# A one-layer diffusion backbone: the opening's sums between its modulation slabs, and linear-attention levels that follow half chunks of weights

## The chip, the cores and the metric

The kernel runs on one core of one Trainium2 chip. A core has a matrix engine (TensorE, PE in the profile; its weight loads are PEld), a vector engine (DVE), a scalar engine (ACT), a general one (GpSimd, POOL) and an engine that mainly issues transfers (SP), and 16 DMA engines. Each engine works through its own queue of instructions in order; semaphores make one wait for another. The metric is the device time of one execution in microseconds (us), and less is better. Before the change it is 1974.27 us, the median of three runs (1974.04 to 1974.33).

## What is computed

One layer for 256 latent tokens and 256 context tokens, 2048 wide, in float32. The reference, cut to what matters here:

```python
mod_x = jnp.split((jax.nn.silu(c) @ w_mod[l] + b_mod[l])[:, None, :], 6, axis=-1)
mod_c = jnp.split((jax.nn.silu(c_ctx) @ w_mod[l] + b_mod[l])[None, None, :], 6, axis=-1)
qa, ka, va, qb, kb, vb, rb, gf, gb, gate_a, gate_b = proj(modulate(x, g_mix[l], mod_x[0], mod_x[1]))
...
o_attn = windowed_attention(qa, ka, va, cka, cva, attn_sink[l])
sf, sb, o_gla_c = context_gla(cqb, ckb, cvb, cgf, cgb, need_out=not last)
o_gla = latent_gla(qb, kb, vb, gf, gb, sf, sb)
x = x + mod_x[2] * merge_branches(o_attn, o_gla, ...)
x = x + mod_x[5] * conv_ffn(modulate(x, g_ffn[l], mod_x[3], mod_x[4]), ...)
```

`modulate` is an RMS norm times (1 + scale) plus shift, and shift and scale come out of `c @ w_mod`. The linear attention (GLA) has 4 heads with 256 key and 512 value channels each, runs in both directions, and decays by log-sigmoid gates (`gf`, `gb`) that are low-rank projections of the normed input.

## The kernel before, in words

**Products.** Each float32 weight is split into a high part (`whi`, on ACT, L211) and a low part (`wlo`, on DVE, L212); activations are split likewise (`h00hi`, `h00lo`: latent tokens, first half of the channels; `h10hi`: context tokens; `h01hi`, `h11hi`: second half). A product is high·high, low·high and high·low. Weights are loaded 1024 columns by 128 rows at a time, a *chunk* of 512 KB (`raw`); a block of projection goes over 16 row tiles in 8 chunks, in `proj_nat` (L222) or `proj_T` (L263). In each chunk PE first runs the products with `whi`, then those with `wlo`.

**Places.** Ahead of a chunk's high part the program calls `tick()` (L171), and ahead of its low part `midway()` (L164) or a function `mid` given in its stead. So a block of 8 chunks has 16 places at which other work is put into PE's queue. A generator in `beside` is stepped there by `aside()` (L156) at a given rate, and small background steps (`bg_steps`) at another. While a place is worked off, `pin` ties its matmuls into PE's order at that place; the order on DVE, ACT and POOL is made by a scheduler with its own model of durations.

**The opening (L538 to L600).** A slab of `w_mod` (`mraw`, 1 MB) is multiplied with the two modulation vectors (`pm`, 32 rows in use), the result is transposed on DVE (`mtr`), turned back into columns by a product (`pcol`), and copied and summed into `scale` or `shift`. `mod_both` (L313) makes such steps: for the first group a0 and a1 are the two slabs of the scale and ea its columns; b0, b1 and eb are those of the shift. `square_sums` (L431) forms the squares of the tokens (`sq`) on ACT and DVE, and `add_up` sums them over channels with a product with ones (`pr`). `factor_row` (L466) makes the norm's factor (`vrow`, `rrow`) of it, `affine_scale` (L497) multiplies tokens, scale and factor into `xr`, and `affine_shift` (L506) adds the shift and splits into `h..hi` (ACT) and `h..lo` (DVE). `idle(n)` (L533) puts n transposes of a constant into PE's queue, whose results nobody reads. The channels come in five groups of 2, 2, 4, 4 and 4 row tiles: (0, 2), (2, 2), (4, 4), (8, 4), (12, 4), and in the loop from L616 each group's normed input goes at once into the blocks QB, KB and VB (partial sums in `qb0`, `kb`, `vb`), while the next groups' slabs are multiplied. In group 1 the function `mid` does so by the list `steps` (how many slab steps each of its six calls takes) and the list `also` (which columns or scales are finished there). SP issues these loads in the order of the program.

**The linear attention (`gla_A`, L740).** For a head four *gate pieces*: a product `pz`, on ACT an absolute value, a relu, an exp and a log (L756 to L760), a sum on DVE (L761, into `segs`) and one on POOL (L762, `gc`). Then eight levels of doubling segments: ACT makes exponentials of the running sums (L829, L830, L836, L837), DVE multiplies them with the head's `q` and `k` (L831, L838) and extends the sums (L840 to L843), and PE multiplies the level before (`pa<-q,k`), which DVE writes into `at` by a mask (L814). Beside some levels stand scans and products for `kf` and `kg` (L770 to L789). At the end two more `q` (L857), the product `pa<-q,kf` and its eviction (`atc`). `with_gla` (L905) steps the whole generator, 4 gate pieces, 8 levels and the end, at rate 0.97 beside the 16 places of a block, which puts the gate pieces at places 1 to 4 and the levels from place 5 on: the block KB for head 0, and a value block (`v_block`) for heads 1 to 3. `gla_o` then multiplies with the values (`po`).

## Time and profile before

| | |
|---|---|
| median of three runs | 1974.27 us (1974.04 to 1974.33) |
| the profiled execution | 1973.72 us, of which the profile's span 1972.0 us |
| PE busy in the span | 99%, 10304 instructions |
| DVE / ACT / POOL busy | 71% / 49% / 2% |
| moved by DMA | 420.90 MB, mean 213 GB/s |
| granted clock of PE | 1.00 |

In a row of a line view stand the start and the length in us, the engine, the line of the kernel, the operation, what it writes and reads, the shapes, how many rows were merged, and in brackets how long the engine stood idle before and for whom. Where one row reads x16 for 8 products of the program, a float32 product that isn't split runs as two passes. Ends of matmuls are modelled, so two starts tell more than an end and a start. Idle time of an engine that nobody waits for costs nothing.

### The profile page before, as it was taken

How to read it: one execution, taken by the hardware profiler on the slowest of the kernel's cores; microseconds unless marked ns; L12 is line 12 of the kernel's file. 1: busy time of each engine (PE TensorE's matmuls, PEld its weight loads, DVE VectorE, ACT ScalarE, POOL GpSimd, SP SyncE). 2: the span in 40 equal slices, each digit the busy share in tenths (PEclk: the TensorE clock that was granted, in tenths of full speed). 3: DMA queues.
4: the chain of work that ended last, by engine and by line, in shares of the span. 5: the costliest groups of instructions: out<-in, count | busy, mean ns of one | idle time of the engine just before them, and what ended most of it. 6: DMA issues, size and time to landing. Idle time of an engine off the chain costs nothing.

```text
span 1972.0 us, 27091 instructions
## 1 busy us (share of the span) xinstructions
PE 1952.8 (99%) x10304; PEld 1635.6 (83%) x10304; DVE 1396.9 (71%) x2150; ACT 971.6 (49%) x1415; POOL 39.9 (2%) x60
## 2 busy tenths in 40 slices
PE   8999999999999999999999999999999999999999
PEld 6679988888887777888888888888888888888887
DVE  5756855785768998777776467989886545677754
ACT  5223655462346565444444445755555334555533
POOL 0010000020000000000000000000000000000000
PEclk9999999999999999999999999999999999999999
DMA  9975222226654466899997677688786556666563
GB/s 392 412 255 176 69 66 71 79 84 210 212 162 126 129 208 220 297 299 307 312 310 237 238 246 252 193 276 284 263 275 224 192 193 191 186 188 191 188 212 114
DMA packets 182867, 420.90 MB, mean 213 GB/s; under 512 B 12512, under 2 KB 12736, under 8 KB 177744
## 3 DMA queue, kind: packets, MB, share of 16 engines
q1 hardware_dynamic: 181200, 413.45, 63.7%
q0 software_dynamic: 1360, 5.54, 1.0%
q8 instruction: 81, 1.33, 0.3%
q14 instruction: 50, 0.41, 0.1%
q10 hardware_dynamic: 176, 0.17, 0.0%
HBM read 416.98 MB, written 2.13 MB: 213 GB/s over the span
## 4 chain that ended last, share of the span: by engine, by line
PE 94%; DVE 3%; ACT 1%; DMA 1%; issue 1%; ACTq 0%; DVEq 0%
PE acc L83 72%; PE accs L83 12%; PE pa L95 2%; PE poa L95 1%; PE pS L95 1%; PE po L95 1%; PE pm L95 1%; DVE wlo L212 1%; PE ptp L98 1%; DMA mraw<-in_w_mod 1%; ACT whi L211 0%; DVE q L831 0%; PE pto L98 0%; DMA pack<-in_k_pack 0%; DVE k L838 0%
## 5 line engine op out<-in xcount | busy, mean ns | idle before, releaser
L212 DVE TENSOR_TENSOR wlo<-raw,whi 128x1024 fp32r<-128x1024 f32 x568 | 694.0, 1223 | 426.5 <-ACT whi L211 387.8
L211 ACT ACTIVATE whi<-raw 128x1024 fp32r<-128x1024 f32 x568 | 601.1, 1059 | 785.1 <-PE acc L83 605.0
L83 PE MATMUL accs<-h,whi 128*128 128x512 f32 x704 | 176.3, 392 | 0.0
L83 PE MATMUL acc<-h,whi 128*128 128x512 f32 x640 | 160.4, 392 | 0.0
L83 PEld LDWEIGHTS accs<-h,whi 128*128 128x128 f32 x704 | 126.6, 189 | 22.6
L83 PE MATMUL acc<-whi,h01hi 128*128 128x512 f32 x352 | 139.7, 397 | 0.0
L83 PE MATMUL acc<-whi,h00hi 128*128 128x512 f32 x352 | 139.2, 395 | 0.0
L83 PE MATMUL acc<-whi,h01lo 128*128 128x512 f32 x352 | 138.4, 393 | 0.0
L83 PE MATMUL acc<-whi,h00lo 128*128 128x512 f32 x352 | 137.6, 391 | 0.0
L83 PE MATMUL acc<-whi,al 128*128 128x512 f32 x352 | 137.0, 389 | 0.0
L83 PE MATMUL acc<-whi,ah 128*128 128x512 f32 x352 | 137.0, 389 | 0.0
L83 PEld LDWEIGHTS acc<-h,whi 128*128 128x128 f32 x640 | 115.1, 189 | 20.6
L83 PEld LDWEIGHTS accs<-h,wlo 128*128 128x128 f32 x704 | 96.0, 190 | 6.9
L83 PE MATMUL acc<-wlo,h01hi 128*128 128x512 f32 x352 | 99.0, 396 | 0.0
L83 PE MATMUL accs<-h,wlo 128*128 128x256 f32 x704 | 98.2, 282 | 0.0
L83 PE MATMUL acc<-wlo,h00hi 128*128 128x512 f32 x352 | 98.1, 394 | 0.0
L83 PE MATMUL acc<-wlo,ah 128*128 128x512 f32 x352 | 94.3, 389 | 0.0
L83 PEld LDWEIGHTS acc<-h,wlo 128*128 128x128 f32 x640 | 87.4, 190 | 6.3
L83 PE MATMUL acc<-h,wlo 128*128 128x256 f32 x640 | 89.4, 282 | 0.0
L376 DVE CUSTOM_DVE_ANT_0 raw<-raw,csrow,pack 128x1024 f32<-128x1024 f32 x64 | 81.2, 1278 | 0.0
L83 PEld LDWEIGHTS acc<-whi,al 128*128 128x128 f32 x352 | 66.1, 188 | 13.7
L83 PEld LDWEIGHTS acc<-whi,ah 128*128 128x128 f32 x352 | 66.1, 188 | 13.7
(376 smaller groups left out, 3553.0 us busy)
## 6 DMA issues: line engine op xcount, KB each, us to landing
raw<-in_w_in SPq DMA_DIRECT2D x204, 512.0 KB, 4.5
raw<-in_w_up SPq DMA_DIRECT2D x176, 512.0 KB, 4.2
raw<-in_w_modT SPq DMA_DIRECT2D x128, 512.0 KB, 4.6
raw<-in_w_down SPq DMA_DIRECT2D x88, 512.0 KB, 3.6
mraw<-in_w_mod SPq DMA_DIRECT2D x30, 1024.0 KB, 12.5
raw<-in_w_attn_o SPq DMA_DIRECT2D x32, 512.0 KB, 5.3
raw<-in_w_gla_o SPq DMA_DIRECT2D x32, 512.0 KB, 5.4
raw<-in_w_out SPq DMA_DIRECT2D x32, 512.0 KB, 4.4
```

The source lines that it names most:

```text
L83: r = pe_seq(PE.matmul(*a, **k))
L95: return pe_seq(after(PE.matmul(*a, **k)))
L98: return pe_seq(after(PE.transpose(*a)))
L211: j = S.activation(hi[:, 0:n, :], raw[:, 0:n, :], AF.Copy).ins
L212: i = V.tensor_tensor(lo[:, 0:n, :], raw[:, 0:n, :], hi[:, 0:n, :].bitcast(F32), op=ALU.subtract).ins
L376: i0 = V.tensor_tensor_reduce(out=raws[i], in0=raws[i], in1=row[0], scale=1.0, scalar=d if h else bmod[:, b0:b0 + 1], op0=ALU.mult, op1=AL ...
```

## The change

Four edits.

1. `mod_both` loads every slab in one transfer; before, the second slab of a first part was loaded in two halves for the first four row tiles.
2. In the opening the products of slab a0 come after four of the nine sums, those of a1 after six, and the factor after all nine. `idle` runs with 10, 2, 4 and 8 transposes instead of 10, 6, 4, 6, 4 and 8. The small `gm1` is tied behind the first square on DVE.
3. In group 1 the list of steps reads 1, 2, 1, 3, 1, 0 instead of 1, 2, 1, 4, 0, 0, and the columns of group 2's shift are finished in the sixth `mid`, ahead of `affine_shift`, instead of the fifth.
4. `gla_A` is split into `gla_gates(h)`, the four gate pieces, and the levels. A table names what stands at each of the 16 places. Head 0: its gates at 0 to 3, levels at 4 and 6 to 13 (the ninth of these steps is the last level's product and the two last `q`), the end at 15. Other heads: their last two gates at 0 and 1, levels at 2, 4, 5, 7, 8, 10, 11, 12 and 13, the end at 15. The next head's first two gate pieces stand at 9 (13 beside head 0) and 14. In the changed file the lines behind the first edit have numbers that differ by a few.

```diff
--- before.py
+++ after.py
@@ -320,12 +320,7 @@
             if k0 == 0:
                 a.append(bank(f"pm{part}_{t0}", (P, w), side=True))
             raw = M("mraw", [P, nk, w])
-            src = A["w_mod01"][part, t0 + k0 // nk].rearrange("p (c d) -> p c d", c=nk)
-            if t0 < 4 and part == 0 and k0:
-                load(raw[:, 0:nk // 2, :], src[:, 0:nk // 2, :])
-                load(raw[:, nk // 2:nk, :], src[:, nk // 2:nk, :])
-            else:
-                load(raw, src)
+            load(raw, A["w_mod01"][part, t0 + k0 // nk].rearrange("p (c d) -> p c d", c=nk))
             for k in range(nk):
                 kt = k0 + k
                 q = 32 * (kt % 4)
@@ -428,6 +423,8 @@
     kbt = M("kb0", [P, 4, 512])
     vb0 = M("vb0", [P, 4, 512])
 
+    squared = []
+
     def square_sums(s):
 
         pr = bank("pr", (P, T), side=True)
@@ -440,7 +437,7 @@
                 if s and i in (0, 2):
                     in_order(evicted[i + 1], j)
             else:
-                V.tensor_tensor(q, x_, x_, op=ALU.mult)
+                squared.append(V.tensor_tensor(q, x_, x_, op=ALU.mult).ins)
                 parts.extend(q[:, k, :] for k in range(4))
                 continue
             h = q[:, 0:2, :]
@@ -538,19 +535,18 @@
     opening[:] = [pe_seq(PE.transpose(warm[:, 0:P], ident, ident)).ins]
     idle(10)
     pr, add_up = square_sums(0)
-    add_up(0, 6)
-    V.tensor_scalar(gm1, gmix, -0.5, None, op0=ALU.mult)
+    add_up(0, 4)
+    in_order(squared[0], V.tensor_scalar(gm1, gmix, -0.5, None, op0=ALU.mult).ins)
     (a0, a1, ea), (b0, b1, eb) = mods[0]
+    a0()
+    add_up(4, 6)
+    a1()
     add_up(6, 9)
     factor_row(pr)
-    a0()
-    idle(6)
-    a1()
-    idle(4)
     ea()
     b0()
     affine_scale(0, *groups[0])
-    idle(6)
+    idle(2)
     b1()
     raws = [first_w(i) for i in range(2)]
     idle(4)
@@ -628,7 +624,7 @@
             bg_rate[:] = [1.4 * len(bg_steps) / ticks + 0.01, 0.0]
             if gi == 1:
                 bg_rate[:] = [0.0, 0.0]
-                steps = iter([1, 2, 1, 4, 0, 0])
+                steps = iter([1, 2, 1, 3, 1, 0])
 
                 def next_columns():
                     if pend:
@@ -639,7 +635,11 @@
                     for s in range(2):
                         affine_scale(s, *groups[2])
 
-                also = iter([next_columns] * 3 + [scale_2, next_columns, lambda: affine_shift(0, *groups[2])])
+                def shift_2():
+                    next_columns()
+                    affine_shift(0, *groups[2])
+
+                also = iter([next_columns] * 3 + [scale_2, next_columns, shift_2])
 
                 def mid():
                     pin[0] = last[0]
@@ -737,16 +737,13 @@
                          b.rearrange("p (f t) -> p f t", f=2), AF.Copy, scale=1.0 / 16)
         return eq
 
-    def gla_A(h, kb, qb, res):
-        k_ = kb[:, (h % 2) * 2:(h % 2) * 2 + 2, 0:T]
-        kc = kb[:, (h % 2) * 2:(h % 2) * 2 + 2, T:2 * T]
-        q_ = qb[:, 2 * h:2 * h + 2, :]
+    def gla_gates(h):
         R = M("segs", [P, 4, 2, T])
-        PF, SB, SX, PX = (R[:, i] for i in range(4))
         G.memset(R[:, 2:4], 0.0)
         gc = []
+        yield R, gc
         for d in range(2):
-            g_ = W2("fc", "gc", [P, 2, T])
+            gc.append(W2("fc", "gc", [P, 2, T]))
             for dt in range(2):
                 f = 2 * h + dt
                 pz = bank("pz", side=True)
@@ -758,11 +755,15 @@
                 S.activation(mn, pz, AF.Relu, scale=-1.0, bias=b)
                 S.activation(e, e, AF.Exp, scale=-1.0)
                 S.activation(e, e, AF.Ln, bias=ones[:, 0:1])
-                V.tensor_tensor((PF if d == 0 else SB)[:, dt, :], mn[:, 0:T], e[:, 0:T], op=ALU.add)
-                G.tensor_tensor(g_[:, dt, :], mn[:, T:2 * T], e[:, T:2 * T], op=ALU.add)
+                V.tensor_tensor(R[:, d, dt, :], mn[:, 0:T], e[:, 0:T], op=ALU.add)
+                G.tensor_tensor(gc[d][:, dt, :], mn[:, T:2 * T], e[:, T:2 * T], op=ALU.add)
                 yield
-            gc.append(g_)
-
+
+    def gla_A(h, kb, qb, R, gc, res):
+        k_ = kb[:, (h % 2) * 2:(h % 2) * 2 + 2, 0:T]
+        kc = kb[:, (h % 2) * 2:(h % 2) * 2 + 2, T:2 * T]
+        q_ = qb[:, 2 * h:2 * h + 2, :]
+        PF, SB, SX, PX = (R[:, i] for i in range(4))
         kf = W2("fb", "kf", [P, 2, T])
         kg = W2("fb", "kg", [P, 2, T])
 
@@ -856,7 +857,6 @@
             S.activation(dst, e, AF.Exp, scale=-1.0 / 16)
             V.tensor_tensor(dst, dst, q_, op=ALU.mult)
         yield
-        yield
         pa = bank("pa", (P, 2, T), side=True)
         for t in range(2):
             for i, (kk, qq) in enumerate(((kf, q2), (kg, q3))):
@@ -902,9 +902,38 @@
     for i in range(4):
         q_evac(i // 2)(i % 2, qb0[i])
 
+    gates = {}
+
+    def gate(h):
+        if h == 4:
+            return
+        if h not in gates:
+            it = gla_gates(h)
+            gates[h] = next(it), it
+        next(gates[h][1])
+
     def with_gla(h, kb, block):
-        res = []
-        beside[:] = [gla_A(h, kb, qbt, res), 0.97, 0.0]
+        res, own = [], []
+
+        def level():
+            if not own:
+                own.append(gla_A(h, kb, qbt, *gates[h][0], res))
+            next(own[0], None)
+
+        this, following = lambda: gate(h), lambda: gate(h + 1)
+        places = {i: [this] for i in ((0, 1, 2, 3) if h == 0 else (0, 1))}
+        for i in (4, 6, 7, 8, 9, 10, 11, 12) if h == 0 else (2, 4, 5, 7, 8, 10, 11, 12):
+            places[i] = [level]
+        places.update({13: [level], 14: [following], 15: [level]})
+        places.setdefault(13 if h == 0 else 9, []).append(following)
+
+        def along():
+            for i in range(16):
+                for fn in places.get(i, ()):
+                    fn()
+                yield
+
+        beside[:] = [along(), 1.0, 0.0]
         v = block()
         for _ in beside[0]:
             pass
```

How the edits move instructions, at three places. First PE's queue in the opening, from the first transposes of a constant (`warm`) to the second slab of the shift; `pr` is a sum of squares, the two `pm` names are scale (first) and shift. Before:

```order
L535 MATMUL warm<-pack 128x128 x10
L462 MATMUL pr<-sq,ones 128x256 x9
L95 MATMUL pm_0_152<-mraw,cS 32x256 x8
L535 MATMUL warm<-pack 128x128 x6
L95 MATMUL pm_0_152<-mraw,cS 32x256 x8
L535 MATMUL warm<-pack 128x128 x4
L95 MATMUL pcol_0_185<-mtr,pack 32x16
L95 MATMUL pm_0_192<-mraw,cS 32x256 x8
L535 MATMUL warm<-pack 128x128 x6
L95 MATMUL pm_0_192<-mraw,cS 32x256 x8
L535 MATMUL warm<-pack 128x128 x4
```

Now:

```order
L532 MATMUL warm<-pack 128x128 x10
L459 MATMUL pr<-sq,ones 128x256 x4
L95 MATMUL pm_0_139<-mraw,cS 32x256 x8
L459 MATMUL pr<-sq,ones 128x256 x2
L95 MATMUL pm_0_139<-mraw,cS 32x256 x8
L459 MATMUL pr<-sq,ones 128x256 x3
L95 MATMUL pcol_0_175<-mtr,pack 32x16
L95 MATMUL pm_0_182<-mraw,cS 32x256 x8
L532 MATMUL warm<-pack 128x128 x2
L95 MATMUL pm_0_182<-mraw,cS 32x256 x8
L532 MATMUL warm<-pack 128x128 x4
```

The slabs of the scale stand between the sums, and 14 transposes ahead of the last slab are gone.

Second DVE's queue from the end of group 1 into group 2: `kb` and `vb` are evictions of group 1's blocks, `mtr` and the copies from `pcol` make group 2's shift, and the `h..lo` are group 2's low parts (the `h00lo` and `h10lo` of channels 4 to 7). Before:

```order
L335 STREAM_TRANSPOSE mtr<-pm_4_693 128x512
L521 TENSOR_TENSOR kb_107<-kb_107,acc 128x512 x4
L345 COPY shift_101<-pcol_4_740 32x2x4 x4
L348 TENSOR_TENSOR shift_101<-shift_101,pack 128x2x4
L212 TENSOR_TENSOR wlo<-raw,whi 128x1024
L512 SCALAR_TENSOR_TENSOR h00lo<-xr_85,shift_101,h00hi 128x256 x4
L521 TENSOR_TENSOR vb_108<-vb_108,acc 128x512 x4
L212 TENSOR_TENSOR wlo<-raw,whi 128x1024
L512 SCALAR_TENSOR_TENSOR h10lo<-xr_87,shift_101,h10hi 128x256 x4
```

Now:

```order
L518 TENSOR_TENSOR kb_107<-kb_107,acc 128x512 x4
L330 STREAM_TRANSPOSE mtr<-pm_4_677 128x512
L340 COPY shift_101<-pcol_4_748 32x2x4 x4
L518 TENSOR_TENSOR vb_108<-vb_108,acc 128x512
L212 TENSOR_TENSOR wlo<-raw,whi 128x1024
L343 TENSOR_TENSOR shift_101<-shift_101,pack 128x2x4
L518 TENSOR_TENSOR vb_108<-vb_108,acc 128x512
L509 SCALAR_TENSOR_TENSOR h00lo<-xr_85,shift_101,h00hi 128x256 x4
L518 TENSOR_TENSOR vb_108<-vb_108,acc 128x512 x2
L509 SCALAR_TENSOR_TENSOR h10lo<-xr_87,shift_101,h10hi 128x256
```

`mtr` has moved behind the four evictions of `kb`, and the shift's copies and sum stand among those of `vb`; ahead of `h00lo` are now two rows of `vb`.

Third the linear attention of head 1, in its late levels. PE's queue there before (`q`, `k` with numbers are those of one level):

```order
L83 MATMUL acc<-wlo,h01hi 128x512 x4
L83 MATMUL acc<-wlo,h11hi 128x512 x4
L83 MATMUL acc<-whi,h01hi 128x512
L83 MATMUL acc<-whi,h01lo 128x512
L95 MATMUL pa<-q_3005,k_3009 128x128 x4
L83 MATMUL acc<-whi,h01hi 128x512
```

and at the corresponding place now:

```order
L83 MATMUL acc<-wlo,h01hi 128x512 x4
L83 MATMUL acc<-wlo,h11hi 128x512 x4
L95 MATMUL pa<-q_2967,k_2971 128x128 x4
L83 MATMUL acc<-whi,h01hi 128x512
L83 MATMUL acc<-whi,h01lo 128x512
```

The level's product stood behind the first two matmuls of a chunk's high part, and now follows the low part of the chunk before directly. DVE's queue for the same levels, before:

```order
L814 COPY_PREDICATED at<-lmask,pa 128x256
L785 TENSOR_TENSOR kf<-kf,kb_107 128x512
L814 COPY_PREDICATED at<-lmask,pa 128x256
L831 TENSOR_TENSOR q_3074<-q_3074,qb 128x512
L840 TENSOR_TENSOR segs<-segs 128x4x64
L838 TENSOR_TENSOR k_3078<-k_3078,kb_107 128x512
L212 TENSOR_TENSOR wlo<-raw,whi 128x1024
L841 TENSOR_TENSOR segs<-segs 128x4x64
L842 TENSOR_TENSOR segs<-segs 128x4x64
```

and now:

```order
L844 TENSOR_TENSOR segs<-segs 128x8x32
L786 TENSOR_TENSOR kf<-kf,kb_107 128x512
L212 TENSOR_TENSOR wlo<-raw,whi 128x1024
L815 COPY_PREDICATED at<-lmask,pa 128x256
L758 TENSOR_TENSOR segs<-gm,ge 128x256
L832 TENSOR_TENSOR q_3071<-q_3071,qb 128x512
L841 TENSOR_TENSOR segs<-segs 128x4x64
L839 TENSOR_TENSOR k_3075<-k_3075,kb_107 128x512
L842 TENSOR_TENSOR segs<-segs 128x4x64
L843 TENSOR_TENSOR segs<-segs 128x4x64
```

The order of the levels' operations is much the same; a sum of the next head's gates (`segs<-gm,ge`) has come between them.

## The prediction

> **What bounds the kernel now.** I read the page's busy table first, then the waits of TensorE (PE) over the whole span (waited for: us in total, times, longest), then busy time by stretches (busy us and count of PE, PEld, DVE, ACT, POOL; granted clock; DMA share; GB/s).

> ```profile
> PE 1952.8 (99%) x10304; PEld 1635.6 (83%) x10304; DVE 1396.9 (71%) x2150; ACT 971.6 (49%) x1415; POOL 39.9 (2%) x60
> ...
> PE pa L95 <- DVE k L838: 2.6, 6, 0.5
> PE pm L95 <- DMA mraw<-in_w_mod: 1.2, 1, 1.2
> PE pa L95 <- DVE q L831: 0.7, 1, 0.7
> ...
> 0.00:20.00 20.00, 12.81 (x99) 8.83 (x103) 8.04 (x22) 6.78 (x9) 0.82 (x5) 1.00 0.91 359
> 40.00:60.00 20.00, 19.43 (x147) 14.01 (x148) 14.43 (x33) 8.33 (x14) 0.00 (x0) 1.00 1.03 414
> ...
> 268.00:334.00 66.00, 65.17 (x323) 54.62 (x322) 42.77 (x83) 37.33 (x76) 4.74 (x5) 1.00 0.22 65
> 334.00:397.00 63.00, 62.20 (x310) 52.07 (x310) 42.77 (x83) 35.56 (x73) 4.74 (x5) 1.00 0.25 76
> 397.00:450.00 53.00, 51.31 (x261) 42.95 (x260) 44.11 (x84) 30.87 (x64) 14.36 (x20) 1.00 0.36 107
> 283.00:299.50 16.50, 16.50 (x90) 14.12 (x90) 16.29 (x37) 8.64 (x22) 0.33 (x1) 1.00 0.22 64
> 299.50:314.00 14.50, 13.67 (x76) 11.28 (x75) 14.09 (x28) 7.71 (x19) 0.95 (x1) 1.00 0.25 75
> ```

> PE is busy 99% of the span, so an edit gains only where PE stands still or works without need. The edits touch two stretches where it stands still. In the first stretch DMA is the limit (share 0.91 and 1.03). In the linear attention of heads 1 to 3 (268 to 450 us) DMA's share is 0.22 to 0.36, and PE misses 0.83 + 0.80 + 1.69 = 3.32 us: just the sum of its waits for `k` (2.6) and `q` (0.7) of the levels. The last two rows say why: in head 1's levels DVE is busy 16.29 of 16.50 and 14.09 of 14.50 us. Over the head it is busy 65% only: the levels' work is bunched.

> **The change, the linear attention.** One product that waits, and the length of a chunk:

> ```profile
> 299.52 0.39 PE L83 MATMUL acc<-whi,h01lo 128*128 128x512 f32 x1
> 299.58 0.69 DVE L838 TENSOR_TENSOR k<-k,kb 128x512 f32<-128x512 f32 x1 [0.29 <-ACT k L837]
> 300.42 1.13 PE L95 MATMUL pa<-q,k 128*128 128x128 f32 x8 [0.51 <-DVE k L838]
> 307.30 0.39 PE L83 MATMUL acc<-whi,h01hi 128*128 128x512 f32 x1
> 308.46 0.79 PE L95 MATMUL pa<-q,k 128*128 128x128 f32 x5 [0.32 <-DVE k L838]
> 315.13 0.40 PE L83 MATMUL acc<-whi,h01hi 128*128 128x512 f32 x1
> ...
> L212 DVE TENSOR_TENSOR wlo<-raw,whi 128x1024 fp32r<-128x1024 f32 x8 | 9.7, 1216 | 8.6 <-ACT ge L756 7.7 <-PE acc L83 0.9
> L756 ACT ACTIVATE ge<-pz,cw 128x512 f32<-128x512 f32 x4 | 2.7, 676 | 0.0
> ```

> PE starts a matmul of the projection at 299.52. The next operation would start 0.23 us later, as the matmuls of a block do; it is the level's product, whose `k` DVE writes only from 299.58, and it starts at 300.42. So 0.90 − 0.23 = 0.67 us are lost where the view prints 0.51 (ends of matmuls are modelled). With this 0.16 more for each of the seven waits they cost 3.3 + 1.1 = 4.4 us.

> A chunk with two products takes 315.13 − 307.30 less the 0.32 + 0.16 lost at 308.46 = 7.35 us, half a chunk 3.7. DVE's work in a head besides the chunks' low parts is 42.77 − 9.7 = 33.1 us, among it head-boundary work that needs no place of its own. Before, a head's levels hang on places 5 to 13: 9 × 3.7 = 33 us, in which 4 to 5 low parts of 1.22 (5.5 us) run too: 38.6 us of work for 33, hence the two full windows. Now they begin at place 2 and reach 13: 12 × 3.7 = 44 us, with 6 low parts 33.1 + 7.3 = 40.4. The load goes from 117% to 92%, and the 3.6 us between them stand against 4.4 us of waits spread over three heads. I take all seven waits away: −4.4.

> Four ACT operations of some 0.68 us make a gate piece, 2.7 us. Two pieces of each next head move into the levels of this one, behind places 9 (13 in head 0) and 14. ACT is busy 37.33 of 66 us, and DVE's sums of them take 0.4 each; ACT has 29 us free in a head, and DVE the 3.6 just found, so I cost them at nothing; uncovered, a piece costs 2.7 (rival B). POOL's part of a piece slows a DVE operation beside it:

> ```profile
> 281.70 0.43 DVE L842 TENSOR_TENSOR segs<-segs 128x256 f32<-128x256 f32 x1 [0.99 <-ACT q L829]
> ...
> 282.36 0.97 POOL L762 TENSOR_TENSOR gc<-gm,ge 128x256 f32<-128x256 f32 x1 [1.04 <-ACT ge L760]
> 282.77 0.84 DVE L841 TENSOR_TENSOR segs<-segs 128x256 f32<-128x256 f32 x1
> ```

> 0.84 beside it, 0.43 for an operation of the same kind and size without it: +0.4 us a piece, inside the slack. [...] POOL (4.74 of 66 us busy) also clears the next head's buffer earlier; it writes only, and nothing is queued behind it.

> What is lost: at three head boundaries an exponential of the next head's levels (0.42 us) now stands on ACT ahead of the final product's eviction `atc` and the splits of v, and waits with them. Bounds 0 and 0.42 each; half of that: +0.6. The linear attention: −4.4 + 0.6 = **−3.8** (bounds −4.4 and −2.2, the latter if half of the waits stay).

> **The opening.**

> ```profile
> 13.07 1.64 PE L462 MATMUL pr<-sq,ones 128*128 128x256 f32 x6 [0.37 <-DVE sq L453]
> 14.64 1.07 PE L95 MATMUL pm<-mraw,cS 128*32 128x256 f32 x16
> 19.14 0.87 PE L535 MATMUL warm<-pack 128*128 128x128 f32 x6
> 19.94 1.07 PE L95 MATMUL pm<-mraw,cS 128*32 128x256 f32 x16
> 23.30 0.39 PE L83 MATMUL acc<-h00hi,whi 128*128 128x256 f32 x1 [0.46 <-ACT h00hi L511]
> 14.75 0.42 DVE L471 TENSOR_SCALAR vrow<-pr 128x256 f32<-128x256 f32 x1 [1.22 <-PE pr L462]
> 19.45 0.88 DVE L502 SCALAR_TENSOR_TENSOR xr<-xr,scale,rrow 128x256 f32<-128x256 f32 x2
> 21.08 0.45 DVE L335 STREAM_TRANSPOSE mtr<-pm 128x256 f32<-128x256 f32 x1 [0.75 <-PE pm L95]
> L104 SPq DMA_DIRECT2D mraw<-in_w_mod x8: 327/376/654, 1.6 to 20.8; - x8
> DMA to landing us min/median/max: 9.8/14.2/17.2
> ```

> Fourteen transposes go (12 ahead of b1 instead of 10 + 6 + 4 + 6 = 26; six took 0.87), and the products of the slabs a0 and a1 move between the sums. But PE does not set the end here: `mtr` of the last slab b1 does, and b1 waits for bytes. The first slab lands at 1.6 + 9.8 = 11.4. At 415 GB/s a slab of 1 MB takes 2.5 us, so b1, three slabs on, lands no sooner than 18.9, and not later than its products started, 19.94. I take 19.5: they move by 0.4. The other chain moves the wrong way: the last sums now follow a1 (lands at 13.9, 1.07 of products), then 1.64 for six: 16.6, 1.9 later than 14.71. From `vrow` to the ready factor are 2.7 us (19.4 instead of 17.5), then `xr` 0.9: 20.3, before `mtr` at 20.7. So **−0.4**; bounds −1.0 and 0 (if the factor is late, DVE is the next in line). The joined load asks for the same bytes with one issue (0.3 us, on a queue that waits): nothing. `gm1`, one small operation, moves on DVE behind the first square, into DVE's wait for the sums (1.22): nothing.

> Group 1's steps:

> ```profile
> 66.52 1.07 PE L95 MATMUL pm<-mraw,cS 128*32 128x512 f32 x8 [1.22 <-DMA mraw<-in_w_mod]
> 67.51 0.38 PE L83 MATMUL acc<-h00hi,wlo 128*128 128x256 f32 x1
> 67.65 0.72 DVE L335 STREAM_TRANSPOSE mtr<-pm 128x512 f32<-128x512 f32 x1 [0.53 <-PE pm L95]
> 68.29 2.48 DVE L521 TENSOR_TENSOR kb<-kb,acc 128x512 f32<-128x512 f32 x4
> 72.66 1.67 DVE L512 SCALAR_TENSOR_TENSOR h00lo<-xr,shift,h00hi 128x256 fp32r<-128x256 f32 x4
> 74.24 2.47 DVE L521 TENSOR_TENSOR vb<-vb,acc 128x512 f32<-128x512 f32 x4
> 76.45 0.39 PE L83 MATMUL acc<-h00hi,whi 128*128 128x256 f32 x1
> ```

> The fourth step waited 1.22 us for its slab, from 65.30 to 66.52, with the low part of `kb`'s block (2.1 us, from 67.51) queued behind it. That low part now goes first: it ends near 65.30 − 0.16 − 0.4 + 2.1 = 66.85, when the slab has landed. So 1.22 + 0.16 = 1.4 us go, and group 2 would start at 76.45 − 1.4 − 0.4 = 74.65.

> Given back: the shift's columns come one mid later, and on DVE the four evictions of `kb` (2.48) now precede `mtr`. By hand, with the rows' durations: evictions 66.9 to 69.4, `mtr` to 70.1, the product `pcol` with its mid near 71.8, copies and one eviction of `vb` (0.62) to 73.1, a low part (1.22) and the columns' sum to 74.5, h00hi 0.43, so h00lo from 74.9 (72.66 before) and PE's first pair from about 75.6. Group 2 starts 0.85 earlier than before, not 1.8, and the 0.4 is in it: **−0.85** for the whole opening. Bounds: −1.8 (both in full) and 0 (the late shift takes it all). Where the slabs limit PE again later, this could be taken back; but at 40 to 60, with DMA at 1.03, PE is busy 19.43 of 20, so it is kept.

> **The sum:** −3.8 − 0.85 = −4.65. The profiled run was 1973.72 us; the median of the runs is 1974.27, 0.55 above. So the profiled execution would take 1973.72 − 4.65 = 1969.07, with a span of about 1967.35 instead of 1972.0, and 1969.6 in the terms of the median.

> **The rivals.** (A) *The waits only move.* The places still have products half a chunk apart (11, 12, 13), and head 3's levels ran into POOL's rotary preparation (14.36 us busy in 397:450), which stays. Half of the waits stay or come back elsewhere: −2.2 + 0.6 − 0.85 = −2.45, 1971.8. Against it: the 92% above; for it: head 3 lost 1.69 of the 3.32.

> (B) *ACT's order holds the levels: slower.* ACT takes its operations in order. A gate piece (2.7 us) whose `pz` stands ahead of a level's exponentials delays the next `whi` and the products. Six pieces: if half of each is uncovered 6 × 1.35 = 8.1 us, 1974.27 − 4.65 + 8.1 = 1977.7; uncovered in full 1985.8. It decides from 4.65/6 = 0.8 us uncovered a piece. Against it: ACT is busy 57% of a head, and before, pieces stood between two heads as well and cost no wait.

> (C) *The clock falls.* b0 lands near 16.4, its products and two transposes end near 17.8, and b1's begin at 19.5: PE now stands still for 1.7 us. The ten early transposes below show the pace of a cold start, 0.23 each against 0.145 for the six at 19.14.

> ```profile
> 6.95 2.34 PE L535 MATMUL warm<-pack 128*128 128x128 f32 x10
> ```

> If that pace came back for as long as this row and half as much again, 3 us of work would take 1.8 more: 1971.4. The waits of PE between 7 and 24 us were 0.46 at the longest in these rows, so no row says that 1.7 is short enough. [...]

> (D) *The opening gives nothing:* 1974.27 − 3.8 = 1970.5.

> **How the numbers follow.** Forecast 0.52, A 0.25, B 0.10, C 0.05, D 0.08. The likeliest's own range: from −6.2 (4.4 + 1.8) to −3.2 (3.2 of the linear attention, nothing of the opening), 1968.1 to 1971.1. The range over all cases reaches 0.5 below that, for group 2's other waits in the opening that I did not follow, and above until no more than B and the tail of A are out: 1967.6 to 1974.6. A measurement here tells 0.2% (3.95 us, the line at 1970.3): the forecast lies 0.7 beyond it, so of its 0.52 some 0.41 are faster and 0.11 within; of A 0.04 and 0.21; of D 0.04 and 0.04; C within; B slower in 0.08 of its 0.10. With a remainder for a mishap that I do not see (0.03 taken from the middle): faster 0.49, within 0.40, slower 0.11.

> **What would show it.** Right: no row "pa <- DVE k" or "<- DVE q" in PE's waits between 200 and 450 us, and DVE below 95% in the late levels of heads 1 and 2; the first projection matmul at 22.9; no "pm <- DMA mraw" near 65 us; the clock at 1.00. Wrong: new PE waits for `whi`, `wlo` or `pa` behind `pz` (B), waits for `k` in head 3 alone (A), first matmuls of group 2 at 76.4 or later (D).

## The result, and the profile after

The changed kernel takes 1967.49 us (median of six runs, 1967.30 to 1968.67), the kernel before in the same series 1974.30 us. The ratio is 0.9967, with a 95% interval of 0.9957 to 0.9978: 6.8 us less, where 4.65 were forecast, and 0.1 below the lower end of the forecast's range (1967.6). The profiled run took 1967.4 us, its span is 1965.6 us instead of 1972.0. That is 6.3 us less: the profiled run of before was 0.6 faster than its median in this series.

First, of the changed kernel, PE's row of the page, the rows of PE's waits that are new or changed, and busy time by stretches (columns as in the prediction); the last two rows are head 1's late levels.

```profile
PE 1950.3 (99%) x10290; PEld 1635.1 (83%) x10290; DVE 1398.9 (71%) x2150; ACT 973.4 (50%) x1415; POOL 37.6 (2%) x60
...
PE pm L95 <- DMA mraw<-in_w_mod: 1.5, 3, 1.0
PE acc L83 <- ACT h00hi L508: 0.7, 2, 0.5
...
268.00:334.00 66.00, 66.00 (x334) 56.14 (x333) 44.84 (x85) 41.60 (x83) 6.40 (x7) 1.00 0.22 65
334.00:397.00 63.00, 63.00 (x317) 53.49 (x316) 44.76 (x87) 37.16 (x75) 4.22 (x5) 1.00 0.25 76
397.00:450.00 53.00, 53.00 (x268) 45.02 (x267) 43.71 (x81) 23.26 (x46) 8.31 (x17) 1.00 0.40 119
281.00:297.50 16.50, 16.50 (x87) 14.09 (x86) 14.17 (x32) 7.96 (x18) 0.00 (x0) 1.00 0.33 97
297.50:312.00 14.50, 14.50 (x82) 12.58 (x81) 12.54 (x26) 9.04 (x19) 0.74 (x1) 1.00 0.25 73
```

PE is busy without a gap from 268 to 450 us; the rows "pa <- DVE k" and "pa <- DVE q" are gone from its waits. DVE is busy 86% in the late levels (14.17 of 16.50, 12.54 of 14.50), where it was 99% and 97%.

To see where the time comes from, it helps to take the same matmul in both traces. I count PE's matmuls of the projections (line 83) and take their starts: the 1st and the 401st (100 us, the opening), counted from the first transpose of the program, and from the 801st to the 2001st (the four heads) and on to the last matmul. The first transpose itself starts when the constants land, between 6.39 and 6.82 us in the fourteen profiles. That is not the kernel's doing: six profiles with the changed opening already span 6.39 to 6.72.

```
                          1st    401st   801st to 2001st   2001st to end
before                   16.62    97.31       300.47          1492.39
changed                  15.66    96.44       294.99          1492.61
```

So in these two traces the heads gave 5.5 us, the opening 0.9 (1.0 already at its first projection matmul) and the start 0.3. Behind the heads the changed kernel's trace is 0.3 longer up to the end of its span, about as much as other profiles differ there. The 0.9 is one profile's figure: three kernels below with the same opening have their 401st matmul at 96.80 to 96.83, which makes it 0.5. Now the opening of the changed kernel, PE and then DVE:

```profile
13.70 1.07 PE L95 MATMUL pm<-mraw,cS 128*32 128x256 f32 x16 [0.28 <-DMA mraw<-in_w_mod]
18.68 1.07 PE L95 MATMUL pm<-mraw,cS 128*32 128x256 f32 x16 [0.96 <-DMA mraw<-in_w_mod]
22.05 0.38 PE L83 MATMUL acc<-h00hi,whi 128*128 128x256 f32 x1 [0.46 <-ACT h00hi L508]
19.03 0.88 DVE L499 SCALAR_TENSOR_TENSOR xr<-xr,scale,rrow 128x256 f32<-128x256 f32 x2
19.83 0.44 DVE L330 STREAM_TRANSPOSE mtr<-pm 128x256 f32<-128x256 f32 x1
```

PE now waits 0.96 us for b1 and starts its products at 18.68 instead of 19.94. DVE ends `xr` just where `mtr` begins: the two chains are even. At the start of group 2, PE and then DVE:

```profile
74.73 0.38 PE L83 MATMUL acc<-h00hi,whi 128*128 128x256 f32 x1 [0.19 <-ACT h00hi L508]
75.25 0.38 PE L83 MATMUL acc<-h00lo,whi 128*128 128x256 f32 x1
75.87 0.28 PE L83 MATMUL acc<-h00hi,whi 128*128 128x256 f32 x1
71.54 0.67 DVE L340 COPY shift<-pcol 32x8 f32<-32x8 f32 x4 [2.56 <-PE pcol L95]
72.84 1.22 DVE L212 TENSOR_TENSOR wlo<-raw,whi 128x1024 fp32r<-128x1024 f32 x1
73.97 0.16 DVE L343 TENSOR_TENSOR shift<-shift,pack 128x8 f32<-128x8 f32 x1
74.71 1.69 DVE L509 SCALAR_TENSOR_TENSOR h00lo<-xr,shift,h00hi 128x256 fp32r<-128x256 f32 x4
```

The chain on DVE is the one that the prediction worked out by hand: columns, an eviction, a low part, the sum (done at 74.1, 74.5 forecast), h00lo at 74.71 (74.9). The third `h00hi` product starts at 75.87; before it stood at 77.03, as far behind the first at 76.45 as a stream without a stop puts it.

### The profile page after: what moved, and what is told of

Read it like the earlier page. It is cut to its first block, busy times and chain, and to the rows that moved or that the text cites. A ratio compares the mean times of both kernels' runs of the same rounds, so it can differ in the third digit from the quotient of the medians.

```text
span 1965.6 us, 27065 instructions
## 1 busy us (share of the span) xinstructions
PE 1950.3 (99%) x10290; PEld 1635.1 (83%) x10290; DVE 1398.9 (71%) x2150; ACT 973.4 (50%) x1415; POOL 37.6 (2%) x60
## 3 DMA queue, kind: packets, MB, share of 16 engines
q8 instruction: 80, 1.31, 0.3%
## 4 chain that ended last, share of the span: by engine, by line
PE 97%; DVE 2%; DMA 1%; ACT 0%; issue 0%; SPq 0%; DVEq 0%
PE acc L83 75%; PE accs L83 13%; PE pa L95 2%; PE poa L95 1%; PE pS L95 1%; PE pm L95 1%; PE po L95 1%; PE ptp L98 1%; DMA mraw<-in_w_mod 1%; DVE wlo L212 1%; PE pto L98 0%; ACT whi L211 0%; PE pz L95 0%; PE plr L608 0%; PE ptx L98 0%
## 5 line engine op out<-in xcount | busy, mean ns | idle before, releaser
L212 DVE TENSOR_TENSOR wlo<-raw,whi 128x1024 fp32r<-128x1024 f32 x568 | 694.1, 1224 | 409.4 <-ACT whi L211 383.5
L83 PE MATMUL accs<-h,whi 128*128 128x512 f32 x704 | 176.3, 392 | 0.0
L83 PE MATMUL acc<-h,whi 128*128 128x512 f32 x640 | 160.4, 392 | 0.0
L83 PEld LDWEIGHTS accs<-h,whi 128*128 128x128 f32 x704 | 126.6, 189 | 22.6
L83 PE MATMUL acc<-whi,h01hi 128*128 128x512 f32 x352 | 139.9, 398 | 0.0
L83 PE MATMUL acc<-whi,h00hi 128*128 128x512 f32 x352 | 139.4, 396 | 0.0
L83 PE MATMUL acc<-whi,h01lo 128*128 128x512 f32 x352 | 138.0, 392 | 0.0
L83 PE MATMUL acc<-whi,h00lo 128*128 128x512 f32 x352 | 137.7, 391 | 0.0
L83 PE MATMUL acc<-whi,al 128*128 128x512 f32 x352 | 137.0, 389 | 0.0
L83 PE MATMUL acc<-whi,ah 128*128 128x512 f32 x352 | 137.0, 389 | 0.0
L83 PEld LDWEIGHTS acc<-h,whi 128*128 128x128 f32 x640 | 115.0, 189 | 20.6
L83 PEld LDWEIGHTS accs<-h,wlo 128*128 128x128 f32 x704 | 96.0, 190 | 6.9
L83 PE MATMUL acc<-wlo,h00hi 128*128 128x512 f32 x352 | 98.2, 395 | 0.0
L83 PE MATMUL acc<-wlo,h01hi 128*128 128x512 f32 x352 | 98.2, 395 | 0.0
L83 PE MATMUL accs<-h,wlo 128*128 128x256 f32 x704 | 98.2, 282 | 0.0
L83 PE MATMUL acc<-wlo,ah 128*128 128x512 f32 x352 | 94.3, 389 | 0.0
L83 PEld LDWEIGHTS acc<-h,wlo 128*128 128x128 f32 x640 | 87.5, 190 | 6.3
L83 PE MATMUL acc<-h,wlo 128*128 128x256 f32 x640 | 89.4, 282 | 0.0
L83 PEld LDWEIGHTS acc<-whi,h00hi 128*128 128x128 f32 x352 | 66.4, 189 | 13.9 <-issue 0.8
L83 PEld LDWEIGHTS acc<-whi,al 128*128 128x128 f32 x352 | 66.1, 188 | 13.7
```

The costliest lines, as they stand in the source:

```text
L83: r = pe_seq(PE.matmul(*a, **k))
L212: i = V.tensor_tensor(lo[:, 0:n, :], raw[:, 0:n, :], hi[:, 0:n, :].bitcast(F32), op=ALU.subtract).ins
```

## The experiments

Each kernel was timed in several rounds beside the kernel before (medians 1973.94 to 1974.04 us in these three series, ranges within 1973.5 to 1974.9). A difference under some 0.4 us between two kernels isn't resolved by the medians.

### Which part gives what

**The heads' edit alone** (kernel before, plus the new `gla_gates`, `gla_A` and `with_gla`):

```diff
-        beside[:] = [gla_A(h, kb, qbt, res), 0.97, 0.0]
+        beside[:] = [along(), 1.0, 0.0]
```

> The kernel before with the linear attention's edit alone. Between 200 and 450 us the changed kernel's matmuls are 5.4 us shorter, start to start: 4.7 at the steps into the levels' products and 0.7 inside them. Theory: that gain is the heads' own and needs nothing of the opening: 1974.3 - 5.4 = 1968.9, and no wait of PE for q or k of a level. Rival: a part of it comes from the earlier end of the opening (the weights' buffers being further ahead), then the gain alone is well below 5 us.

Measured: 1968.35 us (1968.10 to 1969.08), ratio 0.9972 [0.9961, 0.9983], 5.6 less. The stretch of the heads takes 294.91 us, as in the changed kernel, and no wait for `q` or `k` is left. The gain is the heads' own; the rival falls.

**The opening alone** (the joined load, the new order of slabs and sums, the fewer transposes) and **the steps of group 1 alone**:

```diff
-    add_up(0, 6)
+    add_up(0, 4)
...
-    idle(6)
+    idle(2)
     b1()
```

> The kernel before with the joined load and the new order in the opening, without the steps and without the heads' edit. In the profiles the first projection matmul moved from 23.30 to 22.05, 0.28 of it already at the first transpose. Theory: this part gives all that the opening gives, 1.0 us: 1973.3, and the lead of 1.0 at the first projection matmul is still there at 118 us. Rival (the forecast's sizes): 0.4 here, 1973.9, the rest from the steps.

```diff
-                steps = iter([1, 2, 1, 4, 0, 0])
+                steps = iter([1, 2, 1, 3, 1, 0])
```

> The kernel before with group 1's steps and the later shift alone. Theory: the 1.4 us wait for the slab near 65 us goes, and is given back at group 2's start by the late shift on DVE: 1974.3 within 0.3. The forecast's size: 0.45 less, 1973.8. Wait for the slab in the profile: 0.2 or less in both.

Measured: 1973.69 us (1973.30 to 1973.94; ratio 0.9998 [0.9990, 1.0007]) and 1973.94 us (1973.45 to 1975.44; ratio 1.0002 [0.9993, 1.0011]). Alone, neither gives anything that can be told from nothing. In the trace of the first, the 1st projection matmul is 0.97 us earlier (15.65) and the 401st 0.04 (97.27). The rows of PE's waits and timeline near 65 us, in the kernel with the opening alone, say where it went:

```profile
PE pm L95 <- DMA mraw<-in_w_mod: 2.8, 4, 1.4
...
63.69 1.07 PE L95 MATMUL pm<-mraw,cS 128*32 128x512 f32 x8 [0.18 <-DMA mraw<-in_w_mod]
66.17 1.06 PE L95 MATMUL pm<-mraw,cS 128*32 128x512 f32 x8 [1.42 <-DMA mraw<-in_w_mod]
```

The fourth slab's products start at 66.17, against 66.52 before, and that 0.35 is mostly the 0.28 by which all of this profile starts earlier. But for 0.07 us the slab lands as late as before: PE, a microsecond ahead at first, loses most of it in waits for slabs, 0.2 near 37.5 us and the two shown. In the second kernel the wait near 65 us is gone, and the late shift takes its place: the 401st matmul comes 0.17 us earlier. (Four of this kernel's eleven executions took 1975.1 to 1975.4 us, the others at most 1974.2; what sets them apart is open.)

With both edits the 401st matmul comes 0.87 earlier in the changed kernel's profile, and 0.48 to 0.51 in those of three kernels below with the same opening. These wait 0.24 to 0.47 us for the third slab near 64 us, which the changed kernel's profile doesn't. Two kernels with the opening of before lie 0.15 and 0.21 behind its 97.31. So the pair gives 0.5 to 0.9 where the two alone add up to 0.2: more than their sum, but in most profiles by little more than profiles of one opening differ. A reading that fits is that one edit makes PE early and the other lets it use that. My theory that the opening's order carries the gain by itself falls, and the forecast's pair of sizes, 0.4 and 0.45, is not what the parts alone give.

**The changed kernel with the slab's second load in halves**:

```diff
-            load(raw, A["w_mod01"][part, t0 + k0 // nk].rearrange("p (c d) -> p c d", c=nk))
+            src = A["w_mod01"][part, t0 + k0 // nk].rearrange("p (c d) -> p c d", c=nk)
+            if t0 < 4 and part == 0 and k0:
+                load(raw[:, 0:nk // 2, :], src[:, 0:nk // 2, :])
+                load(raw[:, nk // 2:nk, :], src[:, nk // 2:nk, :])
+            else:
+                load(raw, src)
```

> The changed kernel with the second slab of a first part loaded in two halves as before. In the profiles the last slab of the first group landed 3.04 us after the one ahead of it where it came in halves, 2.50 us after in one. Theory: the halves cost 0.5 us of the opening: 1968.0, first projection matmul near 22.5. Rival: the bytes are the same and the 0.5 was other transfers in between, which move with it: 1967.5, first projection matmul near 22.05.

Measured: 1967.86 us (1967.64 to 1968.17), ratio 0.9969 [0.9958, 0.9981]: 0.4 above the changed kernel, between theory and rival, and within what two series differ by. The last slab landed 2.88 us after the one ahead of it, against 2.50 in one load. Its 1st projection matmul was late (16.36 after the first transpose), but not through the halves: PE's slow first stretch lasted longer in this profile (the first eight matmuls of the sums in 3.62 us, 2.41 in that of the changed kernel), so the sums, the factor and `xr` came 0.7 us later. Another kernel below has the load in one and the same 16.36. So this profile can't show what the later slab costs, and by the medians it may be nothing or some 0.4 us: it stays open.

### Why the heads no longer wait

**The levels' places moved back in two steps.** First each head does its four gate pieces at its own places 0 to 3:

```diff
-        places = {i: [this] for i in ((0, 1, 2, 3) if h == 0 else (0, 1))}
-        for i in (4, 6, 7, 8, 9, 10, 11, 12) if h == 0 else (2, 4, 5, 7, 8, 10, 11, 12):
+        places = {i: [this] for i in (0, 1, 2, 3)}
+        for i in (4, 6, 7, 8, 9, 10, 11, 12):
...
-        places.update({13: [level], 14: [following], 15: [level]})
-        places.setdefault(13 if h == 0 else 9, []).append(following)
+        places.update({13: [level], 15: [level]})
```

> The changed kernel with each head's four gate pieces at its own places 0 to 3 and the levels at 4, 6 to 12 and 13 in all heads, none of the next head's pieces early. Products still stand right at the places. Theory: what removed the waits is that the levels have two half chunks more, so DVE has time; taken back, PE waits for k or q again in heads 1 to 3, 1.5 to 4 us in all, 1969 to 1971.5. Rival: it was the products' place at the borders of the parts, then no waits come back and the time is 1967.5.

then, from there, the gates and the first level one place later, where they stood before the change:

```diff
-        places = {i: [this] for i in (0, 1, 2, 3)}
-        for i in (4, 6, 7, 8, 9, 10, 11, 12):
+        places = {i: [this] for i in (1, 2, 3, 4)}
+        for i in (5, 6, 7, 8, 9, 10, 11, 12):
```

> The changed kernel with the table set to the places at which the work stood before: gates at 1 to 4, levels at 5 to 13, the end at 15, nothing of the next head. One half chunk later than the kernel with own gates, which kept all but 0.7 us of the heads' 5.5. Theory: one half chunk of lead makes the difference, so here the waits for q and k are back: 4 us or more, 1971.5 to 1973. Rival: it was the products' pinning at the borders of the parts or the fixed rate: no waits, 1968.3 as with own gates.

Measured: 1968.26 us (1968.12 to 1969.45; ratio 0.9973 [0.9962, 0.9984]) and 1973.43 us (1972.91 to 1973.68; ratio 0.9996 [0.9988, 1.0005]). PE's waits from 195 to 450 us in the first, in one row, and in the second, in two; between them DVE's busy time (third column of times) in head 1's late levels in the first:

```profile
PE pa L95 <- DVE k L839: 0.2, 1, 0.2
...
281.00:297.50 16.50, 16.50 (x91) 14.23 (x90) 16.47 (x37) 9.42 (x22) 0.65 (x1) 1.00 0.31 96
297.50:312.00 14.50, 14.50 (x82) 12.58 (x81) 14.42 (x31) 7.62 (x19) 0.96 (x1) 1.00 0.23 73
...
PE pa L95 <- DVE k L839: 2.6, 6, 0.5
PE pa L95 <- DVE q L832: 0.7, 1, 0.7
```

In its heads the second is the kernel before again, wait for wait, though it is written with the new table: neither the table nor the way it is stepped gains. A stalled product stands again behind the first two matmuls of a high part (298.75 and 298.97, then 299.87); in the first kernel the same product stands ahead of them (298.54). It is due later and waits all the same, so where the product stands isn't what removes the wait. It keeps the changed opening with group 1's steps, and is 0.6 us below the kernel before of its series: that is what these two parts give without the heads. One place's lead of the gates and the first level, 3.7 us, separates it from the first kernel, in which PE waits once. There DVE is as full as ever, 16.47 of 16.50; it only has its backlog before the products are due and not after. The traces show this if one takes, for each of the 28 products of the levels, the time from the end of its `k` on DVE to its start on PE. Before, and in the second kernel, it is 0.15 us in six of them, the six that wait for `k`. With own gates it is 0.36 us or more in all of heads 0 to 2, and down to 0.15 only at the end of head 3, where the one wait is. In the changed kernel it is 1.9 us or more everywhere. The full table brings the heads from 295.70 to 294.99 us and DVE down to 86%. So the forecast's theory (too much of DVE's work in too few places) holds for the cause, with less needed than I wrote: I expected 1.5 to 4 us of waits with one half chunk, and 0.2 was left.

**The old code at rate 1.0**, which also puts everything one place earlier, the late levels with it:

```diff
-        beside[:] = [gla_A(h, kb, qbt, res), 0.97, 0.0]
+        beside[:] = [gla_A(h, kb, qbt, res), 1.0, 0.0]
```

> The kernel before with the rate 1.0 in place of 0.97 and nothing else: everything of a head stands one place earlier, at the same density. Theory (one half chunk of lead): most of the heads' gain with one number, 1969 to 1970. Rival (the levels are too dense, as the forecast had it): the load per half chunk is the same, the waits stay, 1973.5 or more.

Measured: 1977.62 us (1977.20 to 1978.62), ratio 1.0019 [1.0010, 1.0027]: 3.6 us slower than before. Its waits, and one of them, from an execution of 1978.28 us:

```profile
PE pa L95 <- DVE k L838: 4.4, 7, 2.1
PE pa L95 <- DVE q L831: 0.9, 2, 0.5
...
430.99 1.63 PE L95 MATMUL pa<-q,k 128*128 128x128 f32 x8 [2.12 <-DVE k L838]
```

My theory here, that a place's lead is worth most of the gain, falls in this form: an earlier start gains only when the products stay where they are. Here the due places move along, and the waits grow. DVE's work doesn't come earlier by as much as they do: the `k` of each head's first level ends 1.7 to 2.0 us ahead of its product, 3.8 to 4.0 before, and head 0, which had no wait, has 1.0 us. Why one wait reaches 2.1 us I did not find.

**The next head's gate pieces between the densest levels:**

```diff
-        places.update({13: [level], 14: [following], 15: [level]})
-        places.setdefault(13 if h == 0 else 9, []).append(following)
+        places.update({13: [level], 15: [level]})
+        for i in (11, 12):
+            places[i].insert(0, following)
```

> The changed kernel with the next head's two gate pieces at places 11 and 12, both between the late levels, instead of 9 (13) and 14. Theory: ACT and DVE have several us of lead there, and the pieces stay hidden: within 0.5 us, 1967.5 to 1968.0. The forecast's rival B: ACT's 2.7 us a piece hold the exponentials behind them, at least 0.8 us a piece shows, six pieces: 1972 or more, with waits of PE for q, k or whi.

Measured: 1967.69 us (1967.50 to 1967.96), ratio 0.9969 [0.9957, 0.9981]. The heads take 294.95 us and no wait for `q`, `k` or `whi` appears. Rival B, ACT's order, has no price here even between the densest levels.

### What sets the opening

**All sums first, few transposes:**

```diff
-    add_up(0, 4)
+    add_up(0, 6)
...
-    a0()
-    add_up(4, 6)
-    a1()
     add_up(6, 9)
     factor_row(pr)
+    a0()
+    a1()
     ea()
```

> The changed kernel with all nine sums and the factor ahead of the slabs a0 and a1, as before the change, but with the few transposes and the joined load. Theory: in the old order it was the 14 transposes between the slabs that made PE late for b1 (19.94, with its last half landed at 19.50 and in other profiles near 19.0), so dropping them alone is enough: first projection matmul 15.7 us after the first transpose, as in the changed kernel, time 1967.5. Rival: the sums between the slabs are needed, first projection matmul later by up to 0.9, time up to 1968.4.

Measured: 1967.76 us (1967.64 to 1967.94), ratio 0.9969 [0.9956, 0.9981]; the 1st projection matmul 15.96 after the first transpose (15.66 in the changed kernel, 16.62 before). Two thirds of the opening's lead come without the new order, 0.3 from the slabs between the sums. The joined load has no part in the two thirds: the last slab had landed at 19.05, and PE reaches it at 19.39 without a wait. The transposes did stand in the way. What PE waits for here is the scale's columns, 1.28 us at 17.98, because DVE makes the factor ahead of the `mtr` that they need.

**No transposes behind the sums at all:**

```diff
-    idle(2)
     b1()
...
-    idle(4)
     eb()
-    idle(8)
```

> The changed kernel without the 2, 4 and 8 transposes around the last slab of the opening: PE then stands still for up to 1.3 us ahead of b1 and 2.3 us behind it, but for one small product. Theory: the clock does not fall, the first projection matmuls run at the pace as before (0.12 us start to start), and the time is the same within 0.3: 1967.5. Rival C: the clock falls, matmuls take about twice as long for some 3 us, 1969 or more.

Measured: 1969.47 us (1968.84 to 1970.08), ratio 0.9977 [0.9968, 0.9987]: 2.0 above the changed kernel. Stretches of this kernel, and PE around the pauses:

```profile
18.00:22.00 4.00, 1.31 (x18) 0.56 (x18) 3.46 (x14) 1.28 (x2) 0.00 (x0) 0.98 1.00 401
22.00:26.00 4.00, 3.35 (x14) 3.12 (x15) 3.42 (x6) 2.80 (x4) 0.00 (x0) 0.50 1.03 420
26.00:30.00 4.00, 4.00 (x26) 4.00 (x26) 2.15 (x2) 3.06 (x5) 0.00 (x0) 0.66 1.02 424
...
19.11 1.07 PE L95 MATMUL pm<-mraw,cS 128*32 128x256 f32 x16 [1.20 <-DMA mraw<-in_w_mod]
20.93 0.24 PE L95 MATMUL pcol<-mtr,pack 128*32 128x16 f32 x2 [0.75 <-DVE mtr L330]
22.65 0.58 PE L83 MATMUL acc<-h00hi,whi 128*128 128x256 f32 x1 [1.48 <-ACT h00hi L508]
23.76 0.41 PE L83 MATMUL acc<-h00lo,whi 128*128 128x256 f32 x1
23.98 0.41 PE L83 MATMUL acc<-h00hi,whi 128*128 128x256 f32 x1
```

The granted clock falls to 0.50, and matmuls follow at some 0.21 us instead of 0.12 for 6 us. It falls in more than the profiled execution: all ten have a mean clock of 0.998 or 0.999 (0.999 or 1.000 in the changed kernel). My theory falls, and rival C is real: the changed kernel, with a granted clock of 1.00 in all three stretches, stays clear of it because of the 14 transposes behind the sums that it kept.

**Group 2's shift sum ahead of the next low part, on DVE** (`summed` holds the sum of the shift's columns, `hold` what the next `wlo` must follow):

```diff
                 def shift_2():
                     next_columns()
+                    hold.append(summed[0])
                     affine_shift(0, *groups[2])
```

> The changed kernel with one order more on DVE: the sum of group 2's shift columns ahead of the next low part. In the changed kernel the first pairs of group 2 start at 74.73, 75.25 and 75.65, with 0.4 us lost between them and 0.26 ahead. Theory: DVE's order alone makes them late; group 2's first pairs run without a stop, 0.7 us are gained and kept: 1966.8. Rival: slabs and weights still set the pace later, and the lead is gone at 118 us: 1967.5.

Measured: 1968.01 us (1967.52 to 1968.12), ratio 0.9970 [0.9958, 0.9981]: no gain. DVE's rows, and a new wait of PE:

```profile
73.18 1.22 DVE L212 TENSOR_TENSOR wlo<-raw,whi 128x1024 fp32r<-128x1024 f32 x1
75.90 1.87 DVE L518 TENSOR_TENSOR vb<-vb,acc 128x512 f32<-128x512 f32 x3
...
PE acc L83 <- DVE vb L518: 0.5, 1, 0.5
```

The sum is early (73.10), but the low part now pushes three evictions of `vb` behind h00lo, and PE waits for the bank that they free. Neither of my two explanations holds: it isn't the order of the shift and it isn't the loads. From the shift's columns on DVE has more to do than PE gives it time for, whatever comes first.

**The first weights of group 2 split before that stretch**, while DVE has nothing to do (this kernel also has `summed`, without using it):

```diff
                 def shift_2():
+                    early.append(wsplit_raw(wload(w_in[4 * P:6 * P, QB:QB + 512])))
                     next_columns()
                     affine_shift(0, *groups[2])
```

> The changed kernel with the first weights of group 2 split ahead of the shift's columns: DVE stands idle for 2.5 us there (69.0 to 71.5), and the low part of 1.2 us then no longer stands among the shift, h00lo and the evictions of vb. Theory: DVE's own work at the start of group 2 is the limit (with the shift's sum first alone the wait only went over to the evictions of vb), so 0.5 to 0.8 us are gained and kept: 1966.8. Rival: the lead is lost to slabs or weights later, 1967.5.

Measured: 1966.87 us (1966.60 to 1967.41), ratio 0.9965 [0.9951, 0.9978]. That is 0.6 below the median of the changed kernel and 7.2 below the kernel before of its series: the fastest version here, beside the changed kernel at the edge of what is resolved. The trace bears it out, DVE and then PE:

```profile
69.63 1.18 DVE L212 TENSOR_TENSOR wlo<-raw,whi 128x1024 fp32r<-128x1024 f32 x1
72.05 0.67 DVE L340 COPY shift<-pcol 32x8 f32<-32x8 f32 x4 [1.24 <-PE pcol L95]
74.10 1.69 DVE L509 SCALAR_TENSOR_TENSOR h00lo<-xr,shift,h00hi 128x256 fp32r<-128x256 f32 x4
...
74.98 0.39 PE L83 MATMUL acc<-h00hi,whi 128*128 128x256 f32 x1
75.21 0.28 PE L83 MATMUL acc<-h00lo,whi 128*128 128x256 f32 x1
75.33 0.29 PE L83 MATMUL acc<-h00hi,whi 128*128 128x256 f32 x1
```

The low part fills DVE's gap before the columns come, and group 2's pairs run without a stop. From the 201st to the 401st matmul PE takes 37.75 us, 38.54 in the changed kernel and 38.55 to 38.69 in the others with its steps. The 401st comes 96.06 us after the first transpose (96.44), although this profile's 1st was late (16.36).

## Why the prediction was right, and where not

*The bound.* Right: PE stood still for want of `q` and `k`, through DVE, and that is where the time came from (5.5 of the 6.3 us between the traces).

*The heads: −3.8 forecast, −5.5 measured.* "I take all seven waits away: −4.4" held for the mechanism and missed in size. Summed over all pairs of neighbouring matmuls of the heads, start to start, 4.7 us went between the last matmul ahead and the product. Another 0.7 lay inside the products, which run longer after a wait: in the rows of before, 1.13 us for the eight matmuls of the stalled product at 300.42, where a product without a wait takes 1.05. The loss of 0.6 at the head boundaries did not come: the steps from there into `po` are as long as before. The load of 117% and 92% was too high a figure, since boundary work of a head is in the 33.1 us; the trend was right. With own gates the same sum gives ten places, 37 us, for some 39 us of work, an estimate of 105%, and PE waited there for 0.2 us only.

*The opening: −0.85 forecast, −0.9 measured (−0.5 in three other profiles of it): near by luck, with two errors.* "I take 19.5" for b1's landing was the wrong choice in its range: relative to the first transpose its products moved by 0.97, about to the lower bound of 18.9. That the end is set by b1's bytes and not by PE was wrong of the order before (the kernel with sums first and few transposes shows PE late by its transposes) and is right of the changed one. The steps of group 1 were to give another 0.45; alone they gave 0.17, and their use is rather to keep PE's earlier arrival from being lost (the opening alone 0.04, the two together 0.5 to 0.9). The hand-made chain on DVE was good to 0.4 us, but the "first pair from about 75.6" sits where the first pairs, crawling at 0.4 us, in effect put it at 75.3 (75.6 if one adds the 0.3 by which this profile starts earlier).

*The rivals.* A (the waits only move) fell: no wait for `q` or `k` in any head, head 3's included. B fell, with the pieces between the densest levels too. C did not occur in the changed kernel (PE's pause ahead of b1 is 0.96 us, the clock 1.00); without its last 14 transposes it does, for 2.0 us. Its chance of 0.05 was my estimate: no run had shown which pauses keep the clock. D is half right, since the opening gives nothing without the steps, and 0.5 to 0.9 with them. Of the signs, that no slab is waited for near 65 us came true in the changed kernel's profile and not in three others of its opening.

## What to carry to other kernels

When an engine is busy for nearly all of a stretch and idle in the next, ask when its work may start, not how fast it is: half a chunk of lead with the due places held was worth 5 us, and the same lead with the due places moved along cost 3.6. Two edits that each measure as nothing may be a small gain together (0.6 us here): look in the trace of each alone at the first wait behind it, where the lead of the one is lost, and test them together. Take several profiles before you add up tenths of a microsecond: one opening gave a lead of 0.5 in three of them and 0.9 in a fourth. Ahead of a stretch in which an engine is the limit, move into its last gap whatever doesn't depend on what it waits for.

## What the hardware showed

The clock fell with no pause of PE above 2.12 us. Here the stretches of the changed kernel and of the old code at rate 1.0 (from 428.40), in that order:

```profile
18.00:22.00 4.00, 2.91 (x30) 1.83 (x30) 2.94 (x11) 1.57 (x3) 0.00 (x0) 1.00 1.03 410
...
428.40:432.00 3.60, 1.48 (x10) 1.08 (x9) 3.60 (x8) 2.13 (x5) 1.90 (x3) 0.92 0.00 0
432.00:436.00 4.00, 4.00 (x14) 3.28 (x14) 4.00 (x8) 0.97 (x4) 0.00 (x0) 0.64 0.26 80
```

With PE busy 2.91 of 4 us the clock stayed at 1.00. With PE busy 1.31 of 4 us, and the pauses of 1.20, 0.75 and 1.48 shown above (the last reaching beyond the stretch), it fell (0.98 in that stretch, 0.50 in the next), and so it did behind a single wait of 2.12 us in the other kernel (1.48 busy of 3.60; 0.92, then 0.64): the matmuls behind it follow at 0.43 us, where 0.23 is usual, for some 2.5 us. In the kernel without transposes no pause was above 1.48.

The slow first stretch of PE ends at different times from one profile to the next: the first eight matmuls of the sums take 2.41 us in the changed kernel's and 3.62 in those of two kernels whose opening has the same matmuls up to there. In the changed order that delays the factor and with it the first projection matmul by 0.7 us (16.36 instead of 15.66). The granted clock's column reads 1.00 all the while; but the list of the clock's changes begins only at 9.84 us in the changed kernel's trace, and at 12.36 and 12.37 us in the two others'. Up to there the sums' matmuls follow at 0.43 us, behind it at 0.21, a halved pace as in the falls (0.43 against 0.23). So I take it to be the clock, which the column doesn't show there.
